# A decoder layer in one kernel: the norms behind the output projection get a scheduling priority, and the last stage's gain products get buffers of their own

## The chip, the core and the metric

The kernel runs on one core of a Trainium2 chip. Its engines work side by side, each through its own list of instructions in a fixed order: PE (matrix products), DVE (elementwise vector work), ACT (scalar functions and copies), POOL (here: small powers and accumulating DMAs) and SP (starts most DMAs). An instruction that has to wait holds everything behind it on its engine. The metric is the device time of one execution in microseconds (us).

## The reference

The layer has three parts, each between two root-mean-square norms; float32 throughout, 512 tokens of width 1024.

```python
h = h + 0.5 * rmsnorm(swiglu(rmsnorm(h, ffn1_pre_w), ffn1_w_gu, ffn1_w_down), ffn1_post_w)
u = rmsnorm(h, mix_pre_w)
y = token_mixing(u, mem, ..., w_out)          # three gated branches; ends with y @ w_out
h = h + rmsnorm(y, mix_post_w)
h = h + 0.5 * rmsnorm(swiglu(rmsnorm(h, ffn2_pre_w), ffn2_w_gu, ffn2_w_down), ffn2_post_w)

def rmsnorm(x, w):  return x * rsqrt(mean(x * x) + 1e-6) * w
def swiglu(x, w_gu, w_down):
    g, u = split(x @ w_gu, 2)
    return (silu(g) * u) @ w_down
```

The feed-forward width is 2816. The edit touches the seam between `y @ w_out` and the second feed-forward part, and the end of that part.

## The kernel before

**Products.** Each float32 operand is split into a high and a low part (`split`: ACT writes the high part, DVE the rest), and a product is three matmuls: high by high, high by low, low by high. Weights arrive by DMA in stage buffers `st` (4 of them) and are split into buffers `w` (18). A stage buffer is free once its splits are done, a `w` buffer once its last matmul is done. Products go to PSUM banks: `ps` (5 banks), and `px` (3 banks) for transposes and sums off the main line.

**Blocks.** Tokens are cut into four blocks of 128, called 0 to 3 here (`t` in the code), and the width into two halves (`hf`). `out_proj` multiplies first half 0 of the columns for all blocks, then half 1. Behind half 1 of a block comes its chain: ACT squares the product from PSUM, DVE multiplies it by the gain (the gain product, which also frees the bank), DVE adds up the sums of squares (`v`), POOL takes the power (`r`), and DVE updates both halves of h (`postnorm`). Then `prenorm` makes the input of the next part: two squares on ACT, `v`, `r`, two pre-norm products on DVE, two transposes on PE into `px`, and their split into the columns `xhi` and `xlo` that the feed-forward part reads.

**Combinations.** Most of the gate/up products of a feed-forward part work on combinations of quarters of its input (seven products in place of eight, function `pair`). They need the differences and sums `t1` to `t4` of the blocks 0 and 2, and 1 and 3. For that `prenorm` copies transposed blocks out of `px` on ACT (`keep`), and behind blocks 2 and 3 it makes the combinations. A `px` bank is free when split and copy are done. Two of the 22 gate/up column pairs are done plainly ahead of the first combination: `gu_plain`, first for blocks 0 and 1, then for 2 and 3.

**Order.** The code is written as one stream with small tasks in between (`spawn`, `tick`, `need`), which a counter of estimated time wakes. From that stream a scheduler makes each engine's order, after the instructions' priorities, which follow the stream, and the buffers that are free. DMAs on SP are ordered in the same way, so a load may come ahead of another.

**The last stage.** The last four of the 22 row tiles of the down projection are done block by block: PE's product, DVE accumulates it into `y`, ACT squares `y` for the sum, DVE multiplies `y` by the gain in place (so that it waits for the square, which reads `y`), then `v`, `r`, the update of h and the store. Block 3 is cut finer: half 1 in two pieces of 256.

Of the kernel before, what the change touches and what calls it, by code (L numbers as in the profile page):

```python
# [1 line left out]

# [10 lines left out]
ALU = mybir.AluOpType  # L13
# [6 lines left out]
NT = T // P  # L20
# [24 lines left out]
CHUNKS2 = (2, 4, 4, 4, 4, 4)  # L45

LAT = dict(comb=1.0, mem0=0.5, mem1=8.0, mem2=1.5, hg=1.5, hgx=6.0, hg1=6.0, hg2=11.0, hg3=6.0, hg4=6.0, dil0=4.0, dil1=17.0, dil2=5.0,
           dil3=3.0, norm=8.0, mnorm=5.0, mload=10.0, start=0.1, step=2.0, keep=2.0)
PLAN = dict(early1=2, plain1=2, early2=2, plain2=2)
HALVES = (slice(0, 512), slice(512, 1024))  # L50


class Layer:
# [3 lines left out]
    def __init__(self, ctx, tc):  # L57
# [30 lines left out]

        self.strict = False

    def spawn(self, gen):
        task = [0.0, gen, False]
        self.tasks.append(task)
        self.advance(task)
        return task

    def advance(self, task):  # L100
        outer, self.polling = self.polling, True
        try:
            task[0] = self.t + next(task[1])
        except StopIteration:
            task[2] = True
            self.tasks.remove(task)
        self.polling = outer

    def tick(self, us):
        self.t += us  # L110
        while not self.polling:
            due = [x for x in self.tasks if x[0] <= self.t]
            if not due:
                break
            self.advance(min(due, key=lambda x: x[0]))
# [83 lines left out]
    def prenorm(self, src, gain, t, lat, raw):  # L199


        nc = self.nc
        ts = slice(t * P, (t + 1) * P)
        pts = []

        def keep(hf):
            raw[t, hf] = self.slot((P, 4, P))
            nc.scalar.copy(raw[t, hf], pts[hf])

        wait = self.strict and t < 2  # L210
        for x in self.normed(src, gain, lat, self.psum if self.strict and t == 1 else self.paux):
            if isinstance(x, float):
                yield x
                continue
            hf = len(pts)
            pts.append(x)
            self.split(self.xhi[hf][:, :, ts], self.xlo[hf][:, :, ts], x)
            if not wait and (t < 2 or hf == 0):
                keep(hf)
        if wait:  # L220
            def later():
                yield LAT['keep']
                keep(0)
                keep(1)
            self.spawn(later())
        if t < 2:
            return
        ts = slice((t - 2) * P, (t - 1) * P)
        x11, x21, x12 = raw[t - 2, 0], raw[t - 2, 1], raw[t, 0]
        t1, t2, t3 = self.slot((P, 4, P)), self.slot((P, 4, P)), self.slot((P, 4, P))  # L230
        self.tt(t1, x11, x12, ALU.subtract)
        nc.vector.scalar_tensor_tensor(out=t2, in0=t1, scalar=-1.0, in1=pts[1], op0=ALU.mult, op1=ALU.subtract)
        self.tt(t3, x12, pts[1], ALU.subtract)
        for n, x in (("t1", t1), ("t2", t2), ("t3", t3)):
            self.split(self.xc[n][0][:, :, ts], self.xc[n][1][:, :, ts], x)
            yield LAT['comb']
        self.tt(t3, x21, t2, ALU.add)
        self.split(self.xc["t4"][0][:, :, ts], self.xc["t4"][1][:, :, ts], t3)
# [127 lines left out]
    def pair(self, ops):  # L366


        nc = self.nc
        a, cp, cq = self.psum((P, HT)), self.slot(), self.slot()  # L370
        self.product(a, ops, 1)
        nc.scalar.copy(cp[:, :HT], a)
        u, v, p7 = cq[:, :HT], cp[:, HT:], cq[:, HT:]
        b = self.psum((P, HT))
        self.product(b, ops, 6)
        self.tt(u, cp[:, :HT], b, ALU.add)
        c = self.psum((P, HT))
        self.product(c, ops, 5)
        nc.scalar.copy(v, c)  # L379
        d = self.psum((P, HT))  # L380
        self.product(d, ops, 7)
        nc.scalar.copy(p7, d)  # L382
        self.tt(v, p7, v, ALU.subtract)
        self.product(a, ops, 2, False)
        self.product(c, ops, 3, False)
        self.product(d, ops, 4, False)
        return a, u, c, d, v
# [30 lines left out]
            self.mm3(out, (x[k][0][:, ts], x[k][1][:, ts]), w[k], k == 0, k == n - 1)  # L418


    def ffn(self, w_gu, w_down, w_post, ready, reload, after, chunks, early, plain):


        nc = self.nc
        y = [[self.slot() for _ in range(2)] for _ in range(NT)]
# [36 lines left out]
        def down(t, hf, act, ws, first, bank=self.paux, cs=slice(0, 512)):  # L462
            acc = bank((P, cs.stop - cs.start))
            self.proj_N(acc, act, slice(t * P, (t + 1) * P), [(w[0][:, cs], w[1][:, cs]) for w in ws])
            if first:
                nc.scalar.copy(y[t][hf], acc)
            else:
                self.tt(y[t][hf][:, cs], y[t][hf][:, cs], acc, ALU.add)

        tasks, heads = [ready[0]()], []  # L470
# [39 lines left out]
        h = reload()  # L510
        gain = self.bcast_gain(w_post)
        tasks = []
        for t in range(NT):
            whole, parts = slice(0, 512), (slice(0, 256), slice(256, 512))
            ss = []
            for hf in range(2):
                for cs in parts if hf == 1 and t == NT - 1 else (whole,):
                    down(t, hf, act, [w[hf] for w in ws], False, self.psum, cs)
                    ss.append(self.square(y[t][hf][:, cs], hf, 0.5))
                    if len(ss) == 3:  # L520
                        self.tt(ss[1], ss[0], ss[1], ALU.add)
                        del ss[0]
            self.tt(y[t][0], y[t][0], gain[0], ALU.mult)
            r = self.rstd(ss, 0.5)
            self.tt(y[t][1], y[t][1], gain[1], ALU.mult)
            self.postnorm(r, y[t], h[t], parts if t == NT - 1 else (whole,))
            tasks.append(self.spawn(after(h, t)))
# [451 lines left out]
    def out_proj(self, z, w_out, w_post, reload, after):  # L979

        nc = self.nc
        y, ss = [[None, None] for _ in range(NT)], [[None, None] for _ in range(NT)]
        tasks = []
        gain = self.bcast_gain(w_post)
        for hf in range(2):
            w = self.rows(w_out, hf * 512, 512)
            if hf == 1:
                h = reload()
            for t in range(NT):
                ps = self.psum()  # L990
                self.proj_N(ps, z, slice(t * P, (t + 1) * P), w)
                ss[t][hf] = self.square(ps, hf, 1.0)
                y[t][hf] = self.slot()
                self.tt(y[t][hf], ps, gain[hf], ALU.mult)
                if hf == 1:
                    self.postnorm(self.rstd(ss[t], 1.0), y[t], h[t])
                    tasks.append(self.spawn(after(h, t)))
        return tasks


# [7 lines left out]
def layer_kernel(ctx, tc, a, nbias, hmask, out):  # L1008
    nc = tc.nc
    L = Layer(ctx, tc)  # L1010
    x = a["x"][0]

    gpre, raw = [], {}
# [27 lines left out]
    def spill(name):  # L1041
        return [[L.dram.tile([P, T], F32, tag=f"{name}{t}{hf}", name=f"{name}{t}{hf}") for hf in range(2)] for t in range(NT)]

    def reload(src):
        def go():
            h = [[L.slot() for _ in range(2)] for _ in range(NT)]
            for t in range(NT):
                for hf in range(2):
                    L.fetch(h[t][hf], src(t, hf))
            return h  # L1050
        return go

    def follow(dest, w):

        gain, raw = [], {}

        def after(h, t):
            if t == 0:
                gain.extend(L.bcast_gain(w))
            for hf in range(2):  # L1060
                nc.sync.dma_start(out=dest[t][hf], in_=h[t][hf])
            return L.prenorm(h[t], gain, t, LAT['norm'], raw)
        return after

    def store(h, t):
        for c, n in ((0, 512), (512, 256), (768, 256)) if t == NT - 1 else ((0, 512), (512, 512)):
# [3 lines left out]
    h1, h2 = spill("h1"), spill("h2")  # L1070
    ready = L.ffn(a["ffn1_w_gu"][0], a["ffn1_w_down"][0], a["ffn1_post_w"][0], [first, second],
                  reload(lambda t, hf: x[t * P:(t + 1) * P, HALVES[hf]]), follow(h1, a["mix_pre_w"][0]), CHUNKS1, PLAN['early1'], PLAN['plain1'])
    z = L.mixing(a, ready, nbias)
    ready = L.out_proj(z, a["w_out"][0], a["mix_post_w"][0], reload(lambda t, hf: h1[t][hf]), follow(h2, a["ffn2_pre_w"][0]))
    L.ffn(a["ffn2_w_gu"][0], a["ffn2_w_down"][0], a["ffn2_post_w"][0], [lambda: ready[:2], lambda: ready[2:]], reload(lambda t, hf: h2[t][hf]), store, CHUNKS2, PLAN['early2'], PLAN['plain2'])


def constants():
# [39 lines left out]
```

## Time and profile before

| | us |
|---|---|
| median of 3 runs | 1367.82 (1366.94 to 1368.05) |
| the profiled execution | 1367.62 |
| its span, first to last instruction | 1365.8 |
| PE busy in it | 1331.6 (97%) |
| DVE busy | 1050.7 (77%) |
| ACT busy | 742.2 (54%) |

In the profile, L158 and so on are lines of the kernel; where a helper issues an instruction, the line is the helper's. A timeline row has start and duration in us, the engine, the line, the operation, the tiles written and read (without numbers), and in brackets how long the engine was idle ahead of it and what ended that. PE's matmuls overlap, so their issue is read from one start to the next.

### The profile page before, as it was taken

Reading aid. Unit: us, or ns where it says so; the run is one execution under the profiler, and the core shown is the slowest. Engines: PE = TensorE matmul, PEld = TensorE weight load, DVE = VectorE, ACT = ScalarE, POOL = GpSimd, SP = SyncE. Lnnn points to the kernel's source line nnn. Section 1 sums busy time; section 2 is a strip of 40 time slices with the busy share of each in tenths; the row PEclk is TensorE's granted clock in tenths of the full one; section 3 lists DMA queues with packets and bytes.
Section 4 is the critical chain, followed back from the end, with each engine's and each line's share of the span. In section 5 each row is a group of like instructions: output and inputs, shape, how many; then the busy total and the mean of one; then the engine's idle time right before and its main releaser. Section 6 shows DMA issues by size and latency. Waiting matters only on the chain.

```text
span 1365.8 us, 24324 instructions
## 1 busy us (share of the span) xinstructions
PE 1331.6 (97%) x9197; PEld 1233.0 (90%) x9197; DVE 1050.7 (77%) x1996; ACT 742.2 (54%) x1527; POOL 107.0 (8%) x140
## 2 busy tenths in 40 slices
PE   6999999999999999999999999999999999999997
PEld 6999999999789888899899999999889999999996
DVE  6887776777798975598888988897478877677765
ACT  6665544555467655355554755566366655445541
POOL 1111111110100000000000100000011111111100
PEclk9999999999999999999999999999999999999999
DMA  9676565554435335334224333335465765655513
GB/s 271 141 182 184 148 156 142 143 151 125 168 94 177 96 98 163 123 102 117 63 78 124 100 95 93 108 94 154 135 190 135 186 181 151 152 139 148 146 47 139
DMA packets 238123, 185.76 MB, mean 136 GB/s; under 512 B 9109, under 2 KB 198966, under 8 KB 238006
## 3 DMA queue, kind: packets, MB, share of 16 engines
q1 hardware_dynamic: 224246, 160.02, 39.5%
q0 software_dynamic: 12032, 21.04, 9.4%
q10 hardware_dynamic: 1728, 3.15, 0.6%
q8 instruction: 72, 1.18, 0.3%
q14 instruction: 45, 0.37, 0.1%
HBM read 153.73 MB, written 9.47 MB: 119 GB/s over the span
## 4 chain that ended last, share of the span: by engine, by line
PE 87%; DVE 6%; issue 3%; DMA 2%; ACT 1%; POOL 1%; SPq 0%; POOLq 0%; DVEq 0%; ACTq 0%
PE ps L361 17%; PE ps L363 17%; PE ps L362 17%; PE ps L341 6%; PE ps L342 6%; PE ps L343 6%; PE px L341 5%; PE px L342 5%; PE px L343 5%; PE px L348 4%; DVE s L158 2%; PE px L352 1%; DVE w L158 1%; POOL r L181 1%; DVE s L244 1%
## 5 line engine op out<-in xcount | busy, mean ns | idle before, releaser
L161 ACT ACTIVATE w<-sum 128x512 fp32r<-128x512 f32 x288 | 180.2, 631 | 215.9 <-PE ps L362 180.3
L158 DVE TENSOR_TENSOR w<-sum,w 128x512 fp32r<-128x512 f32 x288 | 196.9, 687 | 76.9 <-ACT w L161 75.9
L361 PE MATMUL ps<-xhi,w 128*128 128x256 f32 x864 | 246.3, 285 | 0.9 <-ACT s L379 0.9
L363 PE MATMUL ps<-xhi,w 128*128 128x256 f32 x864 | 244.8, 283 | 0.0
L362 PE MATMUL ps<-xlo,w 128*128 128x256 f32 x864 | 244.4, 283 | 0.0
L161 ACT ACTIVATE w<-st 128x512 fp32r<-128x512 f32 x260 | 162.9, 630 | 126.7 <-PE ps L362 90.0
L158 DVE TENSOR_TENSOR w<-st,w 128x512 fp32r<-128x512 f32 x260 | 177.2, 688 | 39.3 <-ACT w L161 37.9
L158 DVE TENSOR_TENSOR s<-s,s 128x256 f32<-128x256 f32 (+3 forms) x316 | 176.8, 564 | 16.2 <-ACT s L161 4.6
L361 PEld LDWEIGHTS ps<-xhi,w 128*128 128x128 f32 x864 | 165.6, 192 | 3.8 <-ACT s L379 1.2
L362 PEld LDWEIGHTS ps<-xlo,w 128*128 128x128 f32 x864 | 165.6, 192 | 2.4 <-issue 0.2
L363 PEld LDWEIGHTS ps<-xhi,w 128*128 128x128 f32 x864 | 165.5, 192 | 0.0
L158 DVE TENSOR_TENSOR sum<-sum,st 128x512 f32<-128x512 f32 x176 | 120.4, 687 | 10.9 <-issue 5.0
L158 DVE TENSOR_TENSOR s<-s,ps 128x256 f32<-128x256 f32 (+1 forms) x194 | 92.3, 476 | 29.4 <-PE ps L343 24.0
L341 PE MATMUL px<-s,s 128*128 128x512 f32 x288 | 112.6, 391 | 0.0
L342 PE MATMUL px<-s,s 128*128 128x512 f32 x288 | 112.5, 391 | 0.0
L343 PE MATMUL px<-s,s 128*128 128x512 f32 x288 | 112.0, 389 | 0.0
L361 PE MATMUL ps<-t4hi,w 128*128 128x256 f32 x288 | 81.9, 284 | 0.8 <-ACT s L382 0.8
L361 PE MATMUL ps<-t3hi,w 128*128 128x256 f32 x288 | 82.6, 287 | 0.0
L362 PE MATMUL ps<-t3lo,w 128*128 128x256 f32 x288 | 82.0, 285 | 0.0
L361 PE MATMUL ps<-t1hi,w 128*128 128x256 f32 x288 | 81.7, 284 | 0.0
L363 PE MATMUL ps<-t1hi,w 128*128 128x256 f32 x288 | 81.6, 283 | 0.0
L362 PE MATMUL ps<-t2lo,w 128*128 128x256 f32 x288 | 81.5, 283 | 0.0
(186 smaller groups left out, 3344.2 us busy)
## 6 DMA issues: line engine op xcount, KB each, us to landing
st<-in_ffn_w_gu_dram SPq DMA_DIRECT2D x48, 512.0 KB, 4.9
st<-in_w_in_dram SPq DMA_DIRECT2D x48, 512.0 KB, 3.7
st<-in_ffn_w_down_dram SPq DMA_DIRECT2D x44, 512.0 KB, 3.8
sum<-in_ffn_w_gu_dram SPq DMA_DIRECT2D x80, 256.0 KB, 3.4
sh<-in_ffn_w_gu_dram SPq DMA_DIRECT2D x40, 256.0 KB, 3.8
sum<-sh POOLq DMA_DIRECT2D x40, 256.0 KB, 3.6
sum<-st POOLq DMA_DIRECT2D x40, 256.0 KB, 3.3
sum<-in_w_in_dram SPq DMA_DIRECT2D x32, 256.0 KB, 2.9
```

The source lines that it names most:

```text
L158: self.pin(self.nc.vector.tensor_tensor(out=out, in0=a, in1=b, op=op))
L161: self.pin(self.nc.scalar.activation(hi, src, AF.Copy))
L181: self.nc.gpsimd.tensor_tensor(out=r, in0=v, in1=self.mhalf[:, :1], op=ALU.pow)
L244: self.nc.vector.scalar_tensor_tensor(out=h[hf][:, cs], in0=y[hf][:, cs], scalar=r, in1=h[hf][:, cs], op0=ALU.mult, op1=ALU.add)
L341: mm(out, lhsT=lhs[0], rhs=rhs[0], start=first, stop=False)
L342: mm(out, lhsT=lhs[0], rhs=rhs[1], start=False, stop=False)
L343: mm(out, lhsT=lhs[1], rhs=rhs[0], start=False, stop=last)
L348: self.nc.tensor.matmul(out, lhsT=lhsT, rhs=rhs, start=start, stop=stop, **k)
L352: self.nc.tensor.transpose(out, in_, self.ident)
L361: mm(out, lhsT=lh, rhs=rh, start=first and k == 0, stop=False, skip_group_check=True)
L362: mm(out, lhsT=lh, rhs=rl, start=False, stop=False, skip_group_check=True)
L363: mm(out, lhsT=ll, rhs=rh, start=False, stop=k == 3, skip_group_check=True)
```

## The change

The instructions of the norms behind half 1 of the output projection, and every step of the task that follows them (the pre-norm for the next part), are written under a priority that is 300 places earlier than their place in the stream. For this stage alone the copies for the combinations are put off for the blocks 0 and 1 into a later task, the combinations of the blocks 2 and 3 go to tasks of their own without that priority, and `pair` waits for these before its first product. In the last stage the gain product is written into new buffers `z` instead of in place, ahead of `v`.

```diff
+AHEAD = 300
...
     def advance(self, task):
         outer, self.polling = self.polling, True
         try:
-            task[0] = self.t + next(task[1])
+            with self.sooner() if task[3] else nullcontext():
+                task[0] = self.t + next(task[1])
...
+    def sooner(self):
+        return self.tc.high_priority(offset=AHEAD)
...
         wait = self.strict and t < 2
+        behind = not self.strict and self.apart
...
-            if not wait and (t < 2 or hf == 0):
+            if not wait and (t < 2 and not behind or t >= 2 and hf == 0):
                 keep(hf)
-        if wait:
+        if wait or behind and t < 2:
             def later():
                 yield LAT['keep']
                 keep(0)
...
+        if behind:
+            def later():
+                yield LAT['comb']
+                yield from self.combine(raw, pts[1], t)
+            self.combs.append(self.spawn(later()))
+        else:
+            yield from self.combine(raw, pts[1], t)
...
     def pair(self, ops):
+        self.need(*self.combs)
+        self.combs = []
...
+            if last:
+                z = [self.slot() for _ in range(2)]
+                for hf in range(2):
+                    for cs in parts if hf == 1 and t == NT - 1 else (whole,):
+                        self.tt(z[hf][:, cs], y[t][hf][:, cs], gain[hf][:, cs], ALU.mult)
+                self.postnorm(self.rstd(ss, 0.5), z, h[t], parts if t == NT - 1 else (whole,))
+                after(h, t)
+                continue
             self.tt(y[t][0], y[t][0], gain[0], ALU.mult)
...
     def out_proj(...):
-                ss[t][hf] = self.square(ps, hf, 1.0)
-                y[t][hf] = self.slot()
-                self.tt(y[t][hf], ps, gain[hf], ALU.mult)
+                with self.sooner() if hf == 1 else nullcontext():
+                    ss[t][hf] = self.square(ps, hf, 1.0)
+                    y[t][hf] = self.slot()
+                    self.tt(y[t][hf], ps, gain[hf], ALU.mult)
+                    if hf == 1:
+                        self.postnorm(self.rstd(ss[t], 1.0), y[t], h[t])
                 if hf == 1:
-                    self.postnorm(self.rstd(ss[t], 1.0), y[t], h[t])
-                    tasks.append(self.spawn(after(h, t)))
+                    tasks.append(self.spawn(after(h, t), True))
```

What this does to the engines' orders is seen in three places. The first is PE in the output projection, half 1. `ps_12131` is block 2's product; block 3's is `ps_12201` before and `ps_12197` after. Before, block 2 runs through and block 3 follows:

```order
L341 MATMUL ps_12131<-w_12003,s_11799 128x512
L342 MATMUL ps_12131<-w_12004,s_11799 128x512
L343 MATMUL ps_12131<-w_12003,s_11800 128x512
L341 MATMUL ps_12201<-w_11969,s_11205 128x512
L342 MATMUL ps_12201<-w_11970,s_11205 128x512
L343 MATMUL ps_12201<-w_11969,s_11206 128x512
```

After, the end of block 2 stands ahead of the fourth product of the first token half (`ps_12405`) and of block 1's second transpose (`px_12221`); block 3 is done long before, behind block 2's first matmul:

```order
L362 MATMUL ps_12131<-w_12003,s_11799 128x512
L363 MATMUL ps_12131<-w_12004,s_11799 128x512
L364 MATMUL ps_12131<-w_12003,s_11800 128x512
L362 MATMUL ps_12405<-xhi_88,w_12315 128x256
L363 MATMUL ps_12405<-xlo_90,w_12315 128x256
L364 MATMUL ps_12405<-xhi_88,w_12316 128x256
```

Block 2's last nine matmuls moved behind block 3 and behind 36 gate/up matmuls of the blocks 0 and 1.

The second is ACT at the same place. Before, the copies of block 0 out of `px` (`px_12147` and `px_12156`) come ahead of block 2's square:

```order
L161 ACTIVATE xhi_89<-px_12156 128x4x128
L208 COPY s_12154<-px_12147 128x512
L161 ACTIVATE w_12295<-st_12279 128x512
L208 COPY s_12163<-px_12156 128x512
L174 ACTIVATE s_12175,ss_2544_12174<-ps_12131 128x512
L161 ACTIVATE w_12299<-st_12281 128x512
```

After, weight splits (`w_12315` to `w_12640`), block 2's square and the two squares of its updated h (`s_12011`, `s_12012`) come ahead of the copies of block 0 (`px_12147`, `px_12154`) and block 1 (`px_12214`):

```order
L169 ACTIVATE w_12315<-st_12287 128x512
L169 ACTIVATE w_12319<-st_12287 128x512
L169 ACTIVATE w_12640<-st_12617 128x512
L182 ACTIVATE s_12171,ss_2542_12170<-ps_12131 128x512
L182 ACTIVATE s_12184,ss_2547_12183<-s_12011 128x512
L182 ACTIVATE s_12187,ss_2549_12186<-s_12012 128x512
L216 COPY s_12201<-px_12147 128x512
L216 COPY s_12203<-px_12154 128x512
L216 COPY s_12240<-px_12214 128x512
L169 ACTIVATE xhi_89<-px_12221 128x4x128
```

The copies moved behind block 2's norm, and seven weight splits (`w_12299` to `w_12640`) moved ahead of its square. Near it, SP starts the load of `st_12287` ahead of the eight reloads of h and the two loads of the pre-norm gain, where it stood behind them; the stores of the blocks 2 and 3 of h moved behind the next weight loads. On POOL the accumulating DMAs of `sum_12624` and `sum_12634` moved ahead of block 2's first power.

The third is DVE at the end, block 3 of the last stage. Before:

```order
L158 TENSOR_TENSOR s_12277<-s_12277,ps_16469 128x512
L158 TENSOR_TENSOR s_12278<-s_12278,ps_16486 128x256
L158 TENSOR_TENSOR s_12277<-s_12277,s_16333 128x512
L158 TENSOR_TENSOR s_12278<-s_12278,ps_16503 128x256
L158 TENSOR_TENSOR ss_3419_16500<-ss_3416_16483,ss_3419_16500 128x1
L180 TENSOR_SCALAR v_16522<-ss_3419_16500,ss_3422_16517 128x1
L158 TENSOR_TENSOR s_12278<-s_12278,s_16334 128x512
L244 SCALAR_TENSOR_TENSOR s_16323<-s_12277,r_16523,s_16323 128x512
```

After (`s_16333` and `s_16334` are the gain, `s_16527` and `s_16528` the new buffers):

```order
L166 TENSOR_TENSOR s_12277<-s_12277,ps_16475 128x512
L166 TENSOR_TENSOR s_12278<-s_12278,ps_16492 128x256
L166 TENSOR_TENSOR ss_3425_16506<-ss_3422_16489,ss_3425_16506 128x1
L166 TENSOR_TENSOR s_12278<-s_12278,ps_16509 128x256
L166 TENSOR_TENSOR s_16527<-s_12277,s_16333 128x512
L166 TENSOR_TENSOR s_16528<-s_12278,s_16334 128x256 x2
L188 TENSOR_SCALAR v_16532<-ss_3425_16506,ss_3428_16523 128x1
L265 SCALAR_TENSOR_TENSOR s_16323<-s_16527,r_16533,s_16323 128x512
```

All accumulates now come ahead of the gain products, and all gain products ahead of `v`.

More of the change, by code (lines that the diff above doesn't have):

```diff
@@ L1 @@
-from contextlib import ExitStack
+from contextlib import ExitStack, nullcontext
 import concourse.bass as bass
@@ L89, in __init__, with spawn @@
         self.strict = False
-    def spawn(self, gen):
-        task = [0.0, gen, False]
+        self.apart, self.combs = False, []
+    def spawn(self, gen, urgent=False):
+        task = [0.0, gen, False, urgent]
         self.tasks.append(task)
@@ L227, in prenorm, with combine @@
             return
+        if behind:
[5 more added lines that the diff above has]
+            yield from self.combine(raw, pts[1], t)
+    def combine(self, raw, x22, t):
+        nc = self.nc
         ts = slice((t - 2) * P, (t - 1) * P)
@@ L231, in prenorm @@
         self.tt(t1, x11, x12, ALU.subtract)
-        nc.vector.scalar_tensor_tensor(out=t2, in0=t1, scalar=-1.0, in1=pts[1], op0=ALU.mult, op1=ALU.subtract)
-        self.tt(t3, x12, pts[1], ALU.subtract)
+        nc.vector.scalar_tensor_tensor(out=t2, in0=t1, scalar=-1.0, in1=x22, op0=ALU.mult, op1=ALU.subtract)
+        self.tt(t3, x12, x22, ALU.subtract)
         for n, x in (("t1", t1), ("t2", t2), ("t3", t3)):
@@ L418, in proj_N, with ffn @@
             self.mm3(out, (x[k][0][:, ts], x[k][1][:, ts]), w[k], k == 0, k == n - 1)
-    def ffn(self, w_gu, w_down, w_post, ready, reload, after, chunks, early, plain):
+    def ffn(self, w_gu, w_down, w_post, ready, reload, after, chunks, early, plain, last=False):
         nc = self.nc
@@ L1073, in layer_kernel @@
     z = L.mixing(a, ready, nbias)
+    L.apart = True
     ready = L.out_proj(z, a["w_out"][0], a["mix_post_w"][0], reload(lambda t, hf: h1[t][hf]), follow(h2, a["ffn2_pre_w"][0]))
-    L.ffn(a["ffn2_w_gu"][0], a["ffn2_w_down"][0], a["ffn2_post_w"][0], [lambda: ready[:2], lambda: ready[2:]], reload(lambda t, hf: h2[t][hf]), store, CHUNKS2, PLAN['early2'], PLAN['plain2'])
+    L.ffn(a["ffn2_w_gu"][0], a["ffn2_w_down"][0], a["ffn2_post_w"][0], [lambda: ready[:2], lambda: ready[2:]], reload(lambda t, hf: h2[t][hf]), store, CHUNKS2, PLAN['early2'], PLAN['plain2'], True)
 def constants():
```

## The prediction

> **What bounds the kernel now.** I read the page first: the span, and the chain that ended last.
>
> ```profile
> span 1365.8 us, 24324 instructions
> PE 87%; DVE 6%; issue 3%; DMA 2%; ACT 1%; POOL 1%; SPq 0%; POOLq 0%; DVEq 0%; ACTq 0%
> ```
>
> PE carries the chain, so an edit counts where it makes PE wait or lets it go on. Then the busy times by stretch, around the two places that the edit touches. The columns are length, busy PE, PEld, DVE, ACT and POOL with counts, granted clock, DMA share and GB/s.
>
> ```profile
> 980.00:990.00 10.00, 10.00 (x46) 8.29 (x45) 5.33 (x9) 4.25 (x9) 0.12 (x1) 1.00 0.94 294
> 990.00:1000.00 10.00, 10.00 (x49) 8.35 (x49) 5.58 (x10) 3.72 (x11) 1.57 (x3) 1.00 0.82 263
> 1000.00:1010.00 10.00, 8.08 (x47) 6.82 (x46) 7.78 (x15) 7.81 (x20) 2.27 (x3) 1.00 0.37 128
> 1010.00:1020.00 10.00, 9.13 (x75) 8.55 (x74) 9.37 (x17) 6.06 (x15) 3.14 (x5) 1.00 0.73 204
> 1030.00:1330.00 300.00, 300.00 (x2132) 283.35 (x2131) 225.44 (x399) 159.80 (x314) 31.12 (x36) 1.00 0.58 146
> ```
>
> From 1030 to 1330 PE has no idle time at all: whatever it loses or wins at the turn from the output projection to the second feed-forward stage stays until the end. The turn itself shows on PE's timeline:
>
> ```profile
> 993.45 0.39 PE L341 MATMUL ps<-w,s 128*128 128x512 f32 x1
> 993.67 0.39 PE L342 MATMUL ps<-w,s 128*128 128x512 f32 x1
> ...
> 1006.13 0.28 PE L341 MATMUL ps<-xhi,w 128*128 128x256 f32 x1
> 1008.33 0.39 PE L342 MATMUL ps<-xlo,w 128*128 128x256 f32 x1 [1.92 <-DVE xlo L158]
> ...
> 1017.58 0.28 PE L342 MATMUL ps<-xlo,w 128*128 128x256 f32 x1
> 1017.70 0.28 PE L343 MATMUL ps<-xhi,w 128*128 128x256 f32 x1
> 1018.81 0.63 PE L352 MATMUL px<-ident,s 128*128 128x128 f32 x4 [0.83 <-DVE s L190]
> 1019.19 0.36 PE L341 MATMUL ps<-xhi,w 128*128 128x256 f32 x1
> ```
>
> Block 2 (the third of four token blocks) begins its second half at 993.45. A 512-wide matmul takes 0.23 us of issue, a 256-wide one 0.12, four transposes 0.38. PE loses 1008.33 - 1006.13 - 0.12 = 2.1 us and 1018.81 - 1017.70 - 0.12 = 1.0 us: 3.1 us in all. That is the most that the edit could win at the turn.
>
> **The prices.** One norm chain is read from DVE, ACT and POOL:
>
> ```profile
> 992.00 0.63 ACT L174 ACTIVATE s<-s 128x512 f32<-128x512 f32 x1
> 992.76 0.21 DVE L180 TENSOR_SCALAR v<-ss,ss 128x1 f32<-128x1 f32 x1 [0.85 <-ACT s L174]
> 996.64 0.20 DVE L180 TENSOR_SCALAR v<-ss,ss 128x1 f32<-128x1 f32 x1
> 996.99 0.55 POOL L181 TENSOR_TENSOR r<-v,mhalf 128x1 f32<-128x1 f32 x1 [3.38 <-DVE v L180]
> 997.57 1.41 DVE L244 SCALAR_TENSOR_TENSOR s<-s,r,s 128x512 f32<-128x512 f32 x2 [0.73 <-POOL r L181]
> 998.36 0.63 ACT L174 ACTIVATE s<-s 128x512 f32<-128x512 f32 x1 [3.96 <-DVE s L244]
> 1000.55 0.58 ACT L208 COPY s<-px 128x512 f32<-128x512 f32 x1
> 1003.68 0.60 ACT L174 ACTIVATE s<-ps 128x512 f32<-128x512 f32 x1
> 1004.41 0.69 DVE L158 TENSOR_TENSOR s<-ps,s 128x512 f32<-128x512 f32 x1 [0.64 <-ACT s L174]
> 1005.02 0.21 DVE L180 TENSOR_SCALAR v<-ss,ss 128x1 f32<-128x1 f32 x1
> 1005.37 0.86 POOL L181 TENSOR_TENSOR r<-v,mhalf 128x1 f32<-128x1 f32 x1 [4.25 <-DVE v L180]
> 1006.26 1.42 DVE L244 SCALAR_TENSOR_TENSOR s<-s,r,s 128x512 f32<-128x512 f32 x2 [0.44 <-POOL r L181]
> ```
>
> Square to gain product 0.73; product to v 0.61; v to the first update 0.93 with DVE idle, 1.24 with DVE busy (POOL's power takes 0.55 or 0.86); the second update 0.67 later; update to its square 0.79; last square to v 0.76; a copy 0.58. From M, the start of block 2's gain product, this gives: updates at M+1.5 and 2.2, squares to M+3.6, second v at M+3.8, pre-norm products at M+4.7 and 5.4, ready for PE at M+5.5 and 6.2.
>
> **The norm edit moves block 2 back.** No instruction is added at the turn; all that changes is the order. In the new PE order block 2 issues one matmul, then block 3 runs whole; block 2's last nine matmuls stand behind 36 gate/up matmuls of the first token half. After the ninth comes a product that needs block 2's PSUM bank (five ps banks), which its gain product on DVE frees. Three things hang on that.
>
> First the loads. SP now issues a fourth 512 KB weight load ahead of the reloads of h and the pre-norm gain.
>
> ```profile
> 978.65 4.57 DVE L158 TENSOR_TENSOR w<-st,w 128x512 fp32r<-128x512 f32 x7
> 982.31 5.95 SPq L141 DMA_DIRECT2D s<-h  x8
> 988.55 0.98 SPq L141 DMA_DIRECT2D s<-in_ffn_pre_w_dram  x2
> 990.22 0.38 SPq L151 DMA_DIRECT2D st<-in_ffn_w_gu_dram  x1
> 994.71 1.41 DVE L190 SCALAR_TENSOR_TENSOR s<-s,r,s 128x512 f32<-128x512 f32 x2 [1.74 <-DMA s<-in_ffn_pre_w_dram]
> ...
> L151 SPq DMA_DIRECT2D st<-in_ffn_w_gu_dram x1: 383/383/383, 1009.7 to 1009.7; - x1
> ...
> DMA to landing us min/median/max: 3.9/3.9/3.9
> ```
>
> Its stage buffer is free after the seventh split, at 983.2, and 0.5 MB at 294 to 350 GB/s (an estimate from the stretch 980:990 and the eight reloads in 6 us) takes 1.5 us, so block 0's pre-norm starts at 996.2, not 994.7. PE wants that transpose after 12 matmuls, at 996.2, and gets it at 997.0: 0.8 lost. Block 1's chain on DVE now has block 0's lo split ahead of its updates: product 997.5, v 998.1, lo split 998.2, updates 999.4 and 1000.1, v 1001.6, pre-norm product 1002.6, ready 1003.4. PE gets there at 1002.1 (19 matmuls and eight transposes after 997.0): 1.3 lost. Bounds: 0.7 in all if the load delays nothing, 3.5 if it lands as late again. I take 2.1, which the 1.74 us wait on just that gain speaks for.
>
> Second, the bank. PE leaves block 1's transposes at 1003.8, issues 8 wide matmuls, 36 narrow ones and 9 wide ones (17 x 0.23 + 36 x 0.12 = 8.2) and ends block 2 at 1012.0, against about 999.7 before. On ACT the last splits of the stage's weights take buffers that those nine matmuls free, and one more split (a weight load issued near 1007, landing 3.9 later, so just in time) stands ahead of block 2's square. Square 1012.5, M = 1013.25, bank free at M+0.7: 2.0 lost. Bounds: 1.5 without the split ahead, 3.5 if that load lands 1.5 us later.
>
> Third, the px banks. Their three holders are freed by the copies for the combinations; these now stand behind block 2's squares on ACT, so the first ends at M+4.25. PE has 12 matmuls ready (1.4 us, to M+2.2) and then wants a px bank for block 1's other transposes: 2.1 lost. Then block 2's first transposes: ready M+5.5, PE at M+4.7: 0.8. Then 48 narrow matmuls (5.8 us, to M+12.4). Block 3's square stands on ACT behind all that, its product is at M+8.6, its transposes are ready 5.5 later, M+14.1: 1.7 lost. The split of the new columns follows at once: 0.6. (The gaps of 0.1 to 0.3 between transposes, which the old order also has, are left out on both sides.) Together 5.2, bounds 3 and 7: the ready work between the stalls is counted exactly, the chain lengths vary by the 0.3 of each power.
>
> Lost at the turn: 2.1 + 2.0 + 5.2 = 9.3, against 3.1: **+6.2 us**.
>
> The deferred combinations are the same instructions, later, and I cost them at zero: behind the turn PE has 96 narrow matmuls (11.5 us) and then the first pair's products that need no t3, before it wants the late t3 split. Without that cover each late split is 0.7. SP's later stores of h2 have no reader until the last stage. On POOL two accumulating DMAs (0.9 each) now precede block 2's power; the second's source lands near 1012.5, the power is due at M+0.9 = 1014.2.
>
> **The last stage.** Gain products into own buffers wait for no square (one DVE instruction more: block 3's second product comes in two halves), so DVE can do accumulate, accumulate, product, product, v.
>
> ```profile
> 1350.52 0.68 DVE L158 TENSOR_TENSOR s<-s,ps 128x512 f32<-128x512 f32 x1
> ...
> 1356.52 0.28 PE L343 MATMUL ps<-s,s 128*128 128x256 f32 x1
> 1356.66 1.01 DVE L158 TENSOR_TENSOR s<-s,ps 128x512 f32<-128x512 f32 x2
> ...
> 1359.79 0.21 DVE L180 TENSOR_SCALAR v<-ss,ss 128x1 f32<-128x1 f32 x1 [0.57 <-ACT s L174]
> ...
> 1360.14 0.86 POOL L181 TENSOR_TENSOR r<-v,mhalf 128x1 f32<-128x1 f32 x1 [4.86 <-DVE v L180]
> 1361.04 1.54 DVE L244 SCALAR_TENSOR_TENSOR s<-s,r,s 128x512 f32<-128x512 f32 x3 [0.44 <-POOL r L181]
> ```
>
> A block takes DVE 6.1 us (1350.52 to 1356.66), PE only 24 x 0.23 = 5.4, so DVE trails at the end. The new block takes five steps of 0.60, v to update 0.93 and 2 x 0.67: 5.2 us, under PE's pace. The last accumulate can then start when PE is done and the sum of squares is in, near 1357.3 instead of 1358.74; then 0.33 + 0.60 + 2 x 0.33 to v at 1358.9 and 0.93 to the update at 1359.85, against 1361.04: **-1.2 us**. Part of it is the power at 0.55: with v behind the products, DVE is idle then; at 0.86 the gain is about 0.5. [...]
>
> Sum: +6.2 - 1.2 = **+5.0 us** on the profiled execution's 1367.62 (span 1365.8), which lies 0.20 under the median 1367.82: **1372.6 us**.
>
> **The rivals.**
> - *Faster.* Block 2's square comes early enough that PE never runs out of work behind it: both old waits (3.1) and the tail (1.2) are won, 1363.3. It decides at M = 1009.2, when the first copy ends (M+4.25) as PE has done its 12 ready matmuls. Against it: block 2's own last matmul ends only at 1012.0. 5%.
> - *No change that can be told.* What hangs on the px banks costs half of what I think and the gain lands as before: 0.7 + 2.0 + 2.6 - 3.1 - 1.2 = +1.0, 1368.6; with one of the two, 1370. 14%.
> - *A load decides.* The split ahead of block 2's square waits for its load, 2 to 3 us later than I think, and so does everything from M on: 1375. Before, DVE did wait for a load near here (1.74 us). 12%.
> - *The clock drops.* With some 6 us of PE idle within 15, a clock grant lost for one stretch of 3.4 us costs 1.7 more: 1374.2. Against it: the row 1000:1010 holds a 1.92 us wait at clock 1.00, and each new wait is about 2. 4%. [...]
>
> My own case has 65%, its own range 1370.7 to 1374.5. Against no change (0.2%, 2.7 us, is about what a measurement tells): faster 0.05, same 0.14, slower 0.81. The range 1368.7 to 1376.2 leaves out the faster case, some of the no-change case and the far end of the late load.
>
> **What would show it.** In the new profile PE should wait about 2 us at a gate product for DVE's gain product or ACT, 2 us at a transpose for ACT's copy, and 1 to 2 us at transposes for the pre-norm product: 9 to 10 us between 995 and 1030, with the clock at 1.00 and PE full behind it. At the end the last update should follow PE's last matmul by 3.3 us, not 4.5. I am wrong if ACT reaches block 2's square by 1011, if PE's order hides the px wait behind more than 12 matmuls, or if the loads leave the gain where it was.

## The result, and the profile after

The changed kernel takes 1374.96 us (median of 9 runs, 1374.09 to 1379.21), against 1367.82 before in the same measurement: a ratio of 1.0055, 95% interval 1.0042 to 1.0068. That is 7.1 us more. The profiled execution took 1376.44 us, its span is 1374.6 us, 8.8 more than the profiled span before.

The page of the changed kernel, its span and the chain that ended last:

```profile
span 1374.6 us, 24330 instructions
PE 81%; DVE 7%; issue 4%; DMA 4%; ACT 2%; POOL 1%; SPq 0%; DVEq 0%; POOLq 0%; ACTq 0%
```

PE's share of the chain fell from 87% to 81%: the chain now leaves PE more often. The same stretches as before, with one more (length, busy PE, PEld, DVE, ACT and POOL with counts, granted clock, DMA share, GB/s):

```profile
980.00:990.00 10.00, 10.00 (x46) 8.29 (x45) 5.71 (x9) 5.20 (x11) 0.00 (x0) 1.00 0.83 234
990.00:1000.00 10.00, 8.89 (x42) 7.15 (x41) 4.65 (x10) 2.83 (x9) 1.13 (x2) 1.00 0.83 291
1000.00:1010.00 10.00, 9.37 (x57) 7.99 (x56) 7.85 (x13) 5.24 (x11) 1.10 (x2) 1.00 0.37 118
1010.00:1020.00 10.00, 5.89 (x38) 4.74 (x36) 5.34 (x10) 5.28 (x13) 2.87 (x4) 1.00 0.95 252
1020.00:1030.00 10.00, 8.89 (x60) 8.46 (x60) 6.77 (x13) 4.64 (x12) 1.10 (x2) 0.83 0.15 54
1030.00:1330.00 300.00, 298.26 (x2113) 280.97 (x2112) 230.16 (x406) 163.08 (x319) 31.04 (x36) 1.00 0.57 146
```

The loss lies where it was looked for, from 990 to 1030. Two rows say something that the main forecast did not have: the clock of 0.83 in 1020:1030, and 1.7 us without PE in the 300 us behind the turn. PE's timeline names the waits:

```profile
997.14 0.39 PE L363 MATMUL ps<-w,s 128*128 128x512 f32 x1
998.64 0.63 PE L373 MATMUL px<-ident,s 128*128 128x128 f32 x4 [1.11 <-DVE s L198]
...
1003.68 0.40 PE L362 MATMUL ps<-w,s 128*128 128x512 f32 x1
1004.71 0.63 PE L373 MATMUL px<-ident,s 128*128 128x128 f32 x4 [0.63 <-DVE s L198]
...
1013.16 0.39 PE L364 MATMUL ps<-w,s 128*128 128x512 f32 x1
1015.37 0.39 PE L362 MATMUL ps<-xhi,w 128*128 128x256 f32 x1 [1.82 <-DVE s L166]
...
1016.78 0.28 PE L364 MATMUL ps<-xhi,w 128*128 128x256 f32 x1
1019.10 0.66 PE L373 MATMUL px<-ident,s 128*128 128x128 f32 x4 [2.04 <-ACT s L216]
1020.45 1.75 PE L373 MATMUL px<-ident,s 128*128 128x128 f32 x8 [0.69 <-DVE s L198]
...
1028.57 0.28 PE L364 MATMUL ps<-xhi,w 128*128 128x256 f32 x1
1029.51 1.29 PE L373 MATMUL px<-ident,s 128*128 128x128 f32 x8 [0.67 <-DVE s L198]
1030.83 0.38 PE L362 MATMUL ps<-xhi,w 128*128 128x256 f32 x1
1031.56 0.39 PE L363 MATMUL ps<-xlo,w 128*128 128x256 f32 x1 [0.34 <-DVE xlo L166]
...
1074.59 0.28 PE L384 MATMUL ps<-t3hi,w 128*128 128x256 f32 x1
1076.20 0.39 PE L382 MATMUL ps<-xhi,w 128*128 128x256 f32 x1 [1.33 <-ACT s L395]
```

From one start to the next, less the issue of the matmul or of the four transposes ahead (0.23, 0.12, 0.38), PE loses 1.27 at block 0's transposes, 0.80 at block 1's, 1.98 at the bank of block 2 (released by the gain product on DVE), 2.20 at the copy on ACT, 0.97 at block 2's transposes, 0.82 at block 3's, 0.61 at the split behind them, and 1.49 at the first pair's products far behind the turn. The load of the gain, and DVE's wait for it ahead of block 0's pre-norm product, is seen on DVE; below it stand ACT's square of block 2, and on DVE a late weight load, its splits and the gain product that frees the bank:

```profile
997.74 1.41 DVE L198 SCALAR_TENSOR_TENSOR s<-s,r,s 128x512 f32<-128x512 f32 x2 [3.57 <-DMA s<-in_ffn_pre_w_dram]
...
1013.90 0.58 ACT L182 ACTIVATE s<-ps 128x512 f32<-128x512 f32 x1
...
1012.17 0.69 DVE L166 TENSOR_TENSOR sum<-sum,st 128x512 f32<-128x512 f32 x1 [2.75 <-DMA st<-in_ffn_w_gu_dram]
1012.78 1.94 DVE L166 TENSOR_TENSOR w<-st,w 128x512 fp32r<-128x512 f32 x3
1014.63 0.68 DVE L166 TENSOR_TENSOR s<-ps,s 128x512 f32<-128x512 f32 x1
```

The end of the last stage: the last matmul on PE, the last gain products on DVE, the last power on POOL and the last update:

```profile
1366.61 0.28 PE L364 MATMUL ps<-s,s 128*128 128x256 f32 x1
1367.69 1.35 DVE L166 TENSOR_TENSOR s<-s,s 128x512 f32<-128x512 f32 x3
1369.32 0.55 POOL L189 TENSOR_TENSOR r<-v,mhalf 128x1 f32<-128x1 f32 x1 [5.26 <-DVE v L188]
1369.90 1.54 DVE L265 SCALAR_TENSOR_TENSOR s<-s,r,s 128x512 f32<-128x512 f32 x3 [0.73 <-POOL r L189]
```

The last update follows PE's last matmul by 3.29 us, where it was 1361.04 - 1356.52 = 4.52.

### The profile page after: what moved, and what is told of

Its sections match the earlier page's. It is cut to its first block, busy times and chain, and to the rows that moved or that the text cites. A ratio compares the mean times of both kernels' runs of the same rounds, so it can differ in the third digit from the quotient of the medians.

```text
span 1374.6 us, 24330 instructions
## 1 busy us (share of the span) xinstructions
PE 1334.6 (97%) x9197; PEld 1234.2 (90%) x9197; DVE 1051.1 (76%) x1997; ACT 742.9 (54%) x1527; POOL 105.7 (8%) x140
## 4 chain that ended last, share of the span: by engine, by line
PE 81%; DVE 7%; issue 4%; DMA 4%; ACT 2%; POOL 1%; SPq 0%; DVEq 0%; POOLq 0%; ACTq 0%
PE ps L382 15%; PE ps L383 15%; PE ps L384 15%; PE ps L363 6%; PE ps L362 6%; PE ps L364 5%; PE px L362 5%; PE px L363 5%; PE px L364 5%; PE px L369 4%; DVE w L166 2%; DVE s L166 2%; PE px L373 1%; DMA s<-in_ffn_pre_w_dram 1%; POOL r L189 1%
## 5 line engine op out<-in xcount | busy, mean ns | idle before, releaser
L384 PE MATMUL ps<-t2hi,w 128*128 128x256 f32 x288 | 81.5, 283 | 0.0
```

The lines of the kernel that those rows point to most:

```text
L384: mm(out, lhsT=ll, rhs=rh, start=False, stop=k == 3, skip_group_check=True)
```

## The experiments

Each kernel was timed in turn with the kernel before, whose median was 1367.8 to 1368.3 there. Ratios are to it, with 95% intervals.

### The parts of the change, one by one

First the last stage's buffers alone, on the kernel before:

```diff
+            if last:
+                z = [self.slot() for _ in range(2)]
+                ...  # gain products into z, ahead of v
```

> The kernel before with the last stage's own buffers alone: no priority, no deferred copies. My account of the turn (the priority costs there, the buffers save at the end): PE's turn as in the kernel before, 3.1 us lost, and the last update 3.3 us behind PE's last matmul instead of 4.5: 1367.8 - 1.2 = 1366.6. Rival (the buffers do something at the turn too, since more slots are asked for): the turn's waits differ from 3.1. Rival (DVE's pace does not matter): 1367.8.

Measured: 1365.25 us, ratio 0.9981 (0.9967 to 0.9994). In its profile PE waits 1.99 and 0.84 at the turn, where it waited 1.92 and 0.83 before, and the last update follows the last matmul by 1358.39 - 1355.10 = 3.29 us. The buffers win 1.23 us at the end. The median fell by more than the 1.2 I had given, by 3.05; the interval reaches from 0.8 to 4.5. In the two profiles, 2.66 us apart, another 1.28 lies ahead of the turn (block 2's second half begins at 992.17 instead of 993.45), where every engine's order is the same. So 1365.25 may be a low value to compare with.

Then the deferral without the priority:

```diff
     def sooner(self):
-        return self.tc.high_priority(offset=AHEAD)
+        return nullcontext()
```

> The changed kernel without any priority: deferred copies and combinations, and the own buffers. Priority account: most of the loss is gone; what is left is that ACT's and DVE's splits are taken in another order, one or two of 0.6 to 1.0 us that PE then waits for: 1366.6 + 2.0 = 1368.6 (1366.6 to 1370). Deferral account (the copies come late, hold the px banks and so PE, whoever has priority): the px wait of 2.2 us, the transposes of 1.0 and 0.8 behind it and the slower clock (1.5) stay: 1371.5 to 1373.

Measured: 1371.98 us, ratio 1.0032 (1.0021 to 1.0044). The number is that of the deferral account, the mechanism is not: there is no wait for a copy. PE waits elsewhere, for block 0's split columns and for block 3's transposes:

```profile
1004.22 0.39 PE L364 MATMUL ps<-w,s 128*128 128x512 f32 x1
1006.18 0.39 PE L362 MATMUL ps<-xhi,w 128*128 128x256 f32 x1 [1.58 <-ACT xhi L169]
1006.91 0.58 PE L363 MATMUL ps<-xlo,w 128*128 128x256 f32 x1 [0.34 <-DVE xlo L166]
...
1021.39 0.63 PE L373 MATMUL px<-ident,s 128*128 128x128 f32 x4 [1.95 <-DVE s L198]
```

Further waits are 1.11 at a split and 1.37 at the first pair's products, and the granted clock was 0.50 for 3.42 us behind the first of the two rows (1006.79 to 1010.21). My own figure, 1368.6, was 3.4 us too low.

The priority without the deferral:

```diff
-    L.apart = True
```

> The changed kernel without the deferral: copies and combinations stay in the prior tasks; priority 300 and own buffers as they are. Priority account: slower than the changed kernel. The wait for ACT's copy (2.2) goes, but the second transposes of block 1 then stand ahead of the 36 gate/up matmuls and more of these ahead of block 2's last nine, so that block 2 ends later still, and every link behind it (its own transposes, block 3's) is late by more: 1379 (1376 to 1382), with single waits of over 2 us at block 2's and over 4 us at block 3's transposes. Deferral account: 1375.0 less the 2.2 + 1.0 and the slower clock's 1.5 = 1370.3.

Measured: 1379.78 us, ratio 1.0088 (1.0074 to 1.0102). The wait for the copy is gone and the kernel is slower. The wait at block 2's transposes is 1.22, where I had given over 2, the one at its bank 1.81. The row of block 3's transposes:

```profile
1032.35 1.94 PE L373 MATMUL px<-ident,s 128*128 128x128 f32 x8 [4.72 <-DVE s L198]
```

So the px banks held by late copies do not carry the loss: without that wait the kernel is 4.8 us slower. With the own buffers in all four, the medians, from two measurements, are: neither part 1365.25, deferral alone 1371.98, priority alone 1379.78, both 1374.96. The priority costs 14.5 us alone and 3.0 beside the deferral; the deferral costs 6.7 alone and saves 4.8 beside the priority.

### Whose priority it is

The priority for half of the blocks only, in `out_proj` and for the tasks:

```diff
-                with self.sooner() if hf == 1 else nullcontext():
+                with self.sooner() if hf == 1 and t < 2 else nullcontext():
...
-                    tasks.append(self.spawn(after(h, t), True))
+                    tasks.append(self.spawn(after(h, t), t < 2))
```

> The changed kernel with the priority on the norms and pre-norm tasks of token blocks 0 and 1 alone; blocks 2 and 3 have none. Account by the order (the prior transposes of blocks 0 and 1 make the first half's gate/up matmuls ready early, and these overtake block 2's last nine): the whole loss is here, 1375 (1374 to 1376), with the same waits of about 2.0 at the bank and 2.2 at the copy. Rival (each of the four blocks' priority costs its part, or the prior squares of blocks 2 and 3, which stand ahead of the copies, hold the px banks): half of 7.1 or less, about 1371, and no wait for a copy.

The other half has `t > 1` in both places.

> The counterpart of the run with the first two blocks: the changed kernel with the priority on token blocks 2 and 3 alone. Account by the order: block 2's matmuls keep their place, so the waits at its bank (2.0) and for ACT's copy (2.2) are gone; what the deferral alone cost (1372.0) stays, with one more late pair product: 1371.5 (1369 to 1374). Rival (the prior squares and updates of blocks 2 and 3 hold ACT and DVE, and with it the px banks): 1375 or more, with the wait for the copy.

Measured: the first two blocks 1376.16 us (1.0061, 1.0047 to 1.0075), the last two 1372.63 (1.0035, 1.0022 to 1.0048). The first is just above the range I had given. With the first two blocks the changed kernel's waits are back at the same places:

```profile
1013.74 0.39 PE L362 MATMUL ps<-xhi,w 128*128 128x256 f32 x1 [1.87 <-DVE s L166]
...
1017.52 1.12 PE L373 MATMUL px<-ident,s 128*128 128x128 f32 x4 [1.75 <-ACT s L216]
```

With the last two neither is there (the longest wait, 1.92, is for ACT at a gate product, later), and the time is that of the deferral alone within the intervals. So what the priority does in the changed kernel, it does through blocks 0 and 1: they come early, and with them the gate/up matmuls that block 2 then waits behind.

### Block 2's place in PE's order

If block 2's late end carries the loss, holding its place must take most of it away, with the priority as it is. The matmuls of the output projection's second half keep their order among themselves:

```diff
+        if self.hold:
+            mm = lambda *x, **k: self.tc.keep_in_program_order(self.nc.tensor.matmul(*x, **k))
...
+                self.hold = hf == 1
                 self.proj_N(ps, z, slice(t * P, (t + 1) * P), w)
+                self.hold = False
```

First on the kernel with the priority and no deferral, then on the changed kernel:

> The run with priority 300 and no deferral (1379.8), with one thing added: the matmuls of the output projection's second half keep their order among themselves, so that block 3's cannot pass block 2's. Account by the order (block 2's late end carries the loss): the waits at block 2's and block 3's transposes (1.2 and 4.7) and most of the slow clock go: 1370 (1367.5 to 1372.5). Rival (the priority itself loses, by the work that it takes ahead on ACT and DVE): 1378 or more.

> The changed kernel with the same hold on the output projection's second half. Account by the order: the waits at block 2's bank (2.0) and for ACT's copy (2.2) go; block 3's norm, which stands behind the deferred work and 48 matmuls earlier in PE's order, becomes the late one, a single wait of about 4 us at its transposes, and the clock falls behind it: 1372.5 (1370.5 to 1375). Rival (the hold mends the changed kernel as it does the one without deferral): 1368 or less.

Measured: 1370.82 us without deferral (1.0023, 1.0013 to 1.0034), 9.0 less than without the hold; 1373.03 with it (1.0044, 1.0031 to 1.0057), 1.9 less. In the first, no wait at a transpose is over 0.9 us any more; the longest left at the turn is 2.08, for ACT at a gate product. (The profiled execution, 1373.58, is the slowest of its seven; its mean granted clock is 0.996.) In the second the waits at the bank and for the copy are gone, and one at block 3's transposes has taken their place:

```profile
1020.01 0.28 PE L366 MATMUL ps<-xhi,w 128*128 128x256 f32 x1
1024.15 1.94 PE L375 MATMUL px<-ident,s 128*128 128x128 f32 x8 [3.87 <-DVE s L198]
```

So most of what the priority costs goes through the place where block 2 ends: 9.0 of 14.5 us without the deferral, 1.9 of 3.0 beside it. Once that place is held, the deferred order's next late link shows. What is left of the priority's cost behind the hold, 5.6 us against the kernel with the own buffers alone, was not taken apart further.

### The gain's load, and a smaller priority

The pre-norm gain is loaded ahead of the eight reloads of h instead of with block 0's norm; first in the changed kernel, then on the kernel with the own buffers alone:

```diff
             if hf == 1:
+                after.gain()      # loads the pre-norm gain
                 h = reload()
```

> The changed kernel with one thing moved: the pre-norm gain of the second feed-forward stage is loaded ahead of the eight reloads of h, not with block 0's norm. If the late gain is what delays the first transposes (1.1 of the 1.27 us there): block 0's wait goes, 0.8 or so at block 1 may stay, the rest is as it was: 1375.0 - 1.0 = 1374.0 (1373 to 1375), no wait on the gain on DVE. Rival (the late gain shifts the whole chain, block 2's bank and copies too): 1375 less 2 to 3 and a smaller wait at the bank.

> No priority and no deferral: the kernel with the own buffers alone, and the pre-norm gain loaded ahead of the reloads of h. If the late gain (DVE waited 1.74 us for it before) is what makes the lo split late for which PE waited 1.9: that wait shrinks to about 0.5, the later one of 0.8 stays: 1365.3 - 1.5 = 1363.8 (1362.5 to 1365.5). Rival (the gain's wait is covered, the lo split hangs on DVE's work): as with the buffers alone, 1365.3, with the wait of 1.9.

Measured: 1374.52 us in the changed kernel (1.0051, 1.0034 to 1.0068). PE no longer waits at block 0's transposes; the 0.63 at block 1's and the waits of 1.81 and 2.21 stay. So the late gain costs about 1 us there and does not carry the rest; its 0.4 us in the median is less than the measurement can tell. On the kernel with the buffers: 1364.78 us (0.9982, 0.9974 to 0.9990). The 2.0 us that PE lost for a lo split are gone, and the longest wait that the rows name at the turn is 0.36, so the later 0.8, which I had expected to stay, is gone too. The median shows only 0.5 us of this against the buffers alone; why not more is open. DVE finds the gain there:

```profile
993.31 1.41 DVE L190 SCALAR_TENSOR_TENSOR s<-s,r,s 128x512 f32<-128x512 f32 x2 [0.67 <-POOL r L181]
```

The priority at an offset of 20, without the deferral, then with the gain first as well:

> The changed kernel with an offset of 20 instead of 300 and no deferral: a norm may overtake only some 20 instructions, too few for block 0's and 1's transposes to let the 36 gate/up matmuls pass block 2's last nine. Account by the order: block 2 keeps its place and its chain starts earlier; the old wait of 1.9 for a lo split gives way to one of 1.3 at block 1's transposes and the old 0.8 stays: about 1.2 under the kernel with the own buffers alone (1365.25): 1364.0 (1362.5 to 1366). Rival (any priority of the norms moves DVE and ACT away from the splits that PE waits for): 1370 or more.

> The small priority (offset 20, no deferral, own buffers) and the gain ahead of the reloads. If both waits that the small priority has at blocks 0's and 1's transposes (1.0 and 0.65) hang on the gain: 1366.5 - 1.2 = 1365.3 or less, on a level with the gain and buffers alone (within 1.5). Rival (the priority adds something of its own): faster than gain and buffers alone by over 1.5.

Measured: 1366.47 us (0.9985, 0.9974 to 0.9997), a little over what I had given, and 1365.25 (0.9986, 0.9977 to 0.9994). A small priority does no harm, but by these runs it adds nothing to the buffers and the early gain. The version to keep is buffers and early gain: the lowest median of all, 3 us under the kernel before, though not told apart from the buffers alone.

### The clock

The changed kernel's granted clock fell to 0.50 behind its waits of 1.82 and 2.04 us (1020.72 to 1024.13), the kernel before's stayed at 1.00 behind its wait of 1.92. One wait was filled with work:

```diff
+            if self.fill and cs.start == 0:
+                ...  # at the wanted product: its first 12 matmuls once more, ahead of it
             self.proj_T(pu, w[1], self.uT, cs)
```

> The changed kernel with 12 more matmuls: the first half of the product that stands ahead of the wait for ACT's copy is computed twice into the same bank (the second time overwrites it, so the output is the same). 12 x 0.12 = 1.44 us more work for PE, in a wait of 2.2. Clock account (the granted clock falls to 0.50 for about 3.4 us because PE was idle for more than half of the 3.4 us before): the wait becomes 0.8, PE is idle less, the clock stays at 1.00 through 1020 to 1030, and the time falls by the 1.5 us that the slow stretch cost: 1373.5 (1372.5 to 1375). Rival (the clock falls for another reason, or the added work is not covered): 1375 to 1376.5, clock again under 0.9 in that stretch.

Measured: 1374.18 us (1.0044, 1.0028 to 1.0059). The time fits the clock account, the profile does not: the wait for the copy is gone, but in this execution the wait at the bank was 2.74 us, behind DVE's splits of a load that came late, and the clock fell behind that one (0.50 from 1015.54 to 1018.96) and again behind block 3's transposes (0.60 in 1029:1030). As a test of the clock it decides nothing. What says more is where the grant changes. In the changed kernel it falls to 0.50 at 1020.72, is 1.00 again from 1024.13 and falls to 0.50 at 1368.88, behind PE's last matmul: 3.41 and 344.75 us apart, which is 1 and 101 times 3.413. With the priority and no deferral one stretch at 0.50 lasts from 1028.19 to 1038.43, 10.24 us or 3 times 3.413; with the priority on the first two blocks one lasts 6.83 us, from 1014.88 to 1021.71, 2 times. Cut into windows of 3.413 us, counted from such a change in the same trace, the rows below read: start and end, length, PE busy, clock, DMA share, GB/s. The changed kernel, the deferral alone, and the priority without deferral:

```profile
1013.89:1017.30 3.41, 1.69 (x12) 1.00 1.05 237
1017.30:1020.72 3.42, 0.93 (x7) 1.00 0.77 221
1020.72:1024.13 3.41, 3.41 (x19) 0.50 0.00 0
```

```profile
1003.38:1006.79 3.41, 1.61 (x7) 1.00 0.46 150
1006.79:1010.21 3.42, 3.30 (x15) 0.50 0.41 159
```

```profile
1024.78:1028.19 3.41, 1.59 (x11) 1.00 0.14 52
1028.19:1031.61 3.42, 0.00 (x0) 0.50 0.41 153
1031.61:1035.02 3.41, 2.53 (x10) 0.50 0.02 5
1035.02:1038.43 3.41, 3.41 (x17) 0.50 0.00 0
1038.43:1041.85 3.42, 3.42 (x30) 1.00 0.00 0
```

With the end of each execution left out, the rows show eight windows of this length at clock 1.00 in which PE is busy for less than half. Six were followed by one at 0.50: with 0.93 us busy in the changed kernel, 1.61 in the deferral alone and 1.59 in the priority without deferral (the rows above), 1.40 in the filled kernel (1012.13:1015.54), 0.56 in the changed kernel with the hold (1019.73:1023.14), and 1.66 in the kernel with the buffers alone (377.71:381.12). Two were followed by one at 1.00: with 1.69 us in the changed kernel above, and 1.59 with the priority on the last two blocks (1031.80:1035.21; no change of the clock in its rows fixes where its windows begin). So the rows give no threshold: 1.66 us was followed by 0.50 in one trace, 1.69 by 1.00 in another. At 0.50, windows with 3.30 to 3.42 us busy were followed by 1.00, those with 0.00, 2.35 and 2.53 by another at 0.50. In the kernel before the wait of 1.92 us is spread over two windows, and the clock stayed at 1.00 in both and in 1010:1020:

```profile
1004.28:1007.69 3.41, 2.13 (x10) 1.00 0.49 156
1007.69:1011.11 3.42, 2.78 (x22) 1.00 0.45 166
```

It differs between traces far from the edit too, where the code is the same in all kernels: near 380 us the 1.66 us busy in the kernel with the buffers alone were followed by 0.50 (381.12:384.54), 1.94 in the kernel before (379.64:383.05) and 2.37 in the changed kernel (379.01:382.42) by 1.00. That part of the scatter between executions of one kernel comes from where these windows fall is my guess, which no run shows.

## Why the prediction was right

The forecast was 1372.6 in a range of 1368.7 to 1376.2. 1374.96 lies inside that range, but above the 1370.7 to 1374.5 of my own case: the change was 7.1 us, not 5.0. The sign was right, and so was the chain of waits, each at its place. Two terms that the sum left out, the half clock and the late first pair, made the difference, and part of them was hidden by one that came out smaller (block 3's transposes, 0.82 for 1.7). Term by term, in the profiled executions:

| term | forecast | measured |
|---|---|---|
| transposes of blocks 0 and 1 | 0.8 + 1.3 | 1.27 + 0.80 |
| block 2's bank | 2.0 | 1.98 |
| wait for ACT's copy | 2.1 | 2.20 |
| block 2's transposes | 0.8 | 0.97 |
| block 3's transposes, split behind | 1.7 + 0.6 | 0.82 + 0.61 |
| half clock for one window | (a rival, 1.7) | 1.6 |
| late first pair | 0 | 1.5 |
| lost before | -3.1 | -3.1 |
| sum at the turn | +6.2 | +8.7 |
| last stage | -1.2 | -1.2 |

The half-clock row is worked out from PE's starts: from 1020.87 to 1024.26 it issues five transposes and eleven narrow matmuls, 3.39 us where the prices of the prediction give 1.8. The waits that were forecast came to 8.65 instead of 9.3; the half clock and the late first pair add 3.1. That the time still lies in the range is owed to the rivals that had widened it.

From block 2's first matmul to the last one PE needs 371.96 us (994.65 to 1366.61) against 363.07 (993.45 to 1356.52), which is +8.9. Another 1.2 us of the two profiles' 8.8 lies ahead of the turn, where every engine's order is the same; it shows as a wait of 1.44 us for DVE at 723.77, and what brings it about is open.

*The order and the bank.* Right: the runs with the hold and with half of the blocks show that block 2's late end carries most of the priority's cost. The square starts at 1013.90, 0.35 us after PE's last matmul of block 2 has ended, so the load in front of it took almost nothing on ACT. On DVE it was a tie: the splits of a load that came at 1012.17 fill DVE until just when the gain product could start behind the square (1013.90 + 0.73 = 1014.63). So the late-load rival was not decisive here, but by no margin; in the filled kernel's profile it was, with a wait of 2.74.

*The px banks.* The wait is there with its size, 2.20 for 2.1. But as a cause it counts for less than the sum says: taken away with the deferral, it is replaced by worse (1379.78), and taken away by the hold, by one wait of 3.9 us. The terms of such a chain can be added up for one order, not taken out one by one.

*The deferral at zero.* The step that failed is "I cost them at zero". The first pair's products wait 1.5 us for ACT, which stands idle for 3.50 us until 1072.21, for a weight sum on DVE, and then takes splits and other copies ahead of the pair's copy at 1075.78. In the seven traces with the deferral PE loses 0.8 to 1.8 us there, in the seven without it 0.7 at most at any one place. Alone the deferral costs 6.7 us. From the changed kernel's own trace I can show the 1.5; the rest of the 6.7 is put down to the order that the deferral makes without a priority, which was not taken apart.

*The clock.* I gave it 4% and a price of 1.7. The price was about right (1.6), the chance was far too low: of the eleven traces in which PE waits for 1.5 us or more in one go at the turn, seven show a stretch at 0.50 there, in the windows' rows or in narrow matmuls that start 0.21 us apart instead of 0.12 (the changed kernel, the deferral alone, the priority alone, the first two blocks, the gain first, the filled kernel, and the changed kernel with the hold). The prediction shows no row for its stretch of 3.4 us; the changed kernel's rows have one, 0.50 from 1020.72 to 1024.13. The row that I argued from (a 1.92 us wait at clock 1.00) had its wait spread over two windows, with 2.13 and 2.78 us busy. A window need not be idle to be followed by 0.50: 1.61 us busy of 3.41 did not prevent it in the deferral alone. The trace before has such a step at its end: in the window of the last matmul PE was busy for 0.94 us, and the next was at 0.50.

```profile
1355.86:1359.27 3.41, 0.94 (x8) 1.00 0.41 154
1359.27:1362.69 3.42, 0.00 (x0) 0.50 0.01 4
```

*The last stage.* Right: -1.23 for -1.2, with the power at 0.55 us in the last three blocks, where DVE is idle beside it. In the block ahead of these a product on DVE (0.69 us from 1352.13) runs beside the power, and it took 0.94.

## What to carry to other kernels

A priority does not shorten work, it lets some of it pass other work: look for what is passed, and ask who waits for that. Here the norms of the first two blocks came early, and the matmuls they released stood in front of block 2's, on whose end everything behind it hung. When PE waits, count a second price: behind the waits of 1.82 and 2.04 us here the clock was 0.50 for 3.41 us, and the trace before, where it stayed at 1.00 behind 1.92 us, shows one case only.

## What was not expected of the hardware

The changes of the granted clock in the rows above lie whole multiples of 3.413 us apart within a trace (3.41 and 344.75 us in the changed kernel, 6.83 with the priority on the first two blocks, 10.24 with the priority and no deferral). Of the eight windows of this length at clock 1.00 in which PE was busy for 0.56 to 1.69 us, six were followed by one at 0.50; at 0.50, windows with 2.35 and 2.53 us busy were followed by another, and those with 3.30 to 3.42 by 1.00. So a wait of 1.6 to 2 us may cost some 1.7 us more (an estimate, half of 3.41; 1.6 in the changed kernel's trace) or nothing (the kernel before, 1.92 us). In the kernel with priority and no deferral the stretch of 10.24 us at 0.50 took in three windows, with 0.00, 2.53 and 3.41 us busy.
